# Half of the down projection by seven block products for eight, and a quarter of the up projection's low weight parts by ScalarE and an accumulating transfer

## The chip, the core and the metric

The kernel runs on one core of a Trainium2 chip. The metric is the device time of one launch in microseconds (us). Names used below: PE is the matrix engine TensorE, PEld its weight load, DVE is VectorE, ACT is ScalarE, POOL is GpSimd, SP is SyncE, which issues the loads. SBUF is the memory on the chip that all engines work from, PSUM the memory that matmuls write to.

## The reference, cut to what matters

Two layers, 256 tokens, model width 2048, hidden width 5632, all in float32:

```
x = x + group outputs @ w_out          # two kinds of attention, not touched here
h = rms_norm(x, g2)
u = h @ w_up                           # 2048 -> 2 x 5632 (gate and value)
u = depthwise conv of width 3 over the tokens, per channel, plus bias
m = silu(u[gate]) * u[value]           # 256 x 5632
x = x + m @ w_down                     # 5632 -> 2048
```

The change touches the last line (the down projection), the intermediate m, and the way in which a part of w_up is made ready.

## The kernel before, in words

**Three products for one.** PE multiplies in a format with fewer bits than float32 (fp32r). So each float32 operand is split into a high part, which ACT writes as a rounded copy (L104, in `split`), and a low part, which DVE writes as the difference of the operand and its high part (L105). A product is then high by high, plus low by high, plus high by low. `three` (L388) issues these for the projections in which the tokens' tile is PE's stationary operand and the weights, 512 columns wide, move past it; `two` is the form of the up projection, in which the weights are stationary and a 512-wide matmul (both parts of the activations) is followed by a 256-wide one (the weights' low part).

**Steps.** All weights pass through one pipe. They arrive as tiles of 1 MB (`raw`, 128 partitions by 2048), one tile a *quantum*, by SP's queue in three buffers (`load`); a quantum has two halves, each a *step*: 128 by 1024 weights, split by one instruction on ACT (`whi`) and one on DVE (`wlo`), used by 12 matmuls of `three` or 16 of `two`. `whi` and `wlo` have five buffers each; `split_w` is called four steps ahead of the matmuls. The load of a later quantum goes into a `raw` buffer when the last split of the quantum in it is done.

**Order in a layer.** Input projection, attention, output projection; then the hidden width, cut into 44 tiles of 128 (f = 0 to 43), in chunks (`CHUNKS`, 12, 12, 12 and 8 tiles). For every f of a chunk the up projection takes two quanta (u = 0, 1; 64 matmuls) and `glu` follows: ACT copies the PSUM result (L505), DVE adds its second half (L506) and scales by the norm into a `halo` tile (L507), POOL copies the tile's edges (L509, L510), ACT and DVE do the convolution (L515, L517, four times), ACT the SiLU (L519), DVE the gate (L520), and `split` makes `mid`, the high and low part of m's tile. A chunk's down projection comes after the up projection of the *next* chunk's first tile, so that a `glu` runs beside matmuls that do not need its result; it goes over four column blocks nb of 512, for each over the chunk in groups of four tiles (`q_down`), and adds the PSUM sum to the residual `x` on DVE (`add_x`, L453). In the last chunk of 8, behind which there is no up projection, the order is sorted: both column blocks nb = 0, 1 take the first four tiles, then both take the last four.

**What sets the order.** The program is written as one list of steps, and a scheduler (Tile) orders each engine's instructions by a cost model and by priorities; `split_w` has a raised priority, and so has the last `glu`. Each engine then works through its own list in that order, and waits at an instruction until its inputs and its output buffer are ready. PSUM has 8 banks: two tiles of two banks under the name mm, two of one bank under S, and one each of one bank under tr and pv.

Of the kernel before, what the change touches and what calls it, by code (L numbers as in the profile page):

```python
# [11 lines left out]
F32 = mybir.dt.float32  # L12
# [21 lines left out]
CHUNKS = (12, 12, 12, 8)  # L34
# [17 lines left out]
def encoder_kernel(  # L52
# [91 lines left out]
    def stat_x(which):  # L144
        v = work.tile([P, TT], F32, name="ssum", bufs=2)
        nc.vector.reduce_sum(v, st["ss"], axis=AX.X)
        st["r1"] = act.tile([P, TT], F32, name="r1")
        rsqrt(v, 1.0 / D, st["r1"], "c2")
        if which == 1:

            d = work.tile([P, 4, HD], F32, name="tq", bufs=2)
            for tt in range(TT):
                nc.vector.tensor_scalar(d[:, tt], ident, st["r1"][:, tt:tt + 1], None, op0=ALU.mult)
            ps = psum.tile([P, T], F32, name="pv", bufs=1)
            mm(ps, ones, d[:, 0:TT].rearrange("p t d -> p (t d)"), True, True)
            st["r2"] = act.tile([P, T], F32, name="r2")
            nc.scalar.activation(st["r2"], ps, AF.Copy)
# [199 lines left out]
    def values(l, grp, h):  # L357
# [14 lines left out]
        os[k] = act.tile([P, 2, T], F32R, name="mid", bufs=16)  # L372
# [128 lines left out]
    def glu(l, f, ps):  # L501
# [49 lines left out]
    for l in range(L):  # L551
        for j in range(NJ):
            for u in range(4):
                quanta.append((a["w_in"][l, j, u], q_win(l, j, u), False))
        for grp in "ba":
            for nb in range(NB):
                for u in range(2):
                    quanta.append((a["w_out"][l, 0 if grp == "a" else 1, nb, u], q_wout(l, grp, nb, u), False))
        f = 0
        for c, nf in enumerate(CHUNKS):  # L560

            end = min(sum(CHUNKS[:c + 1]) + 1, NF)
            while f < end:
                for u in range(2):
                    quanta.append((a["w_up"][l, f, u], q_up(l, f, u), True))
# [13 lines left out]
    def load(q, parts=1):  # L579
        if q < len(quanta):  # L580
            raw[q] = wp.tile([P, 2048], F32, name="raw", bufs=3)
            left[q] = 2
# [3 lines left out]

    def split_w(s, parts=1):
        if s < len(steps):
            q, half = steps[s]
            at_ = UP_AT if quanta[q][2] else 0  # L590
            hl[s] = tuple(wp.tile([P, 1024 + 64], F32R, name=t, bufs=SPLIT_AHEAD + 1)[:, at_:at_ + 1024]
                          for t in ("whi", "wlo"))
            m = 1024 // parts
            for j in range(parts):
                with tc.high_priority(offset=AHEAD_PRIO if s >= KD // 2 else 0):
                    highs[s] = split(*(t[:, j * m:(j + 1) * m] for t in hl[s]),
                                     raw[q][:, half * 1024 + j * m:half * 1024 + (j + 1) * m])
# [7 lines left out]
    for i in range(KD // 2):  # L605
        xT.append(act.tile([P, 2, T], F32, name="mid", bufs=16))
# [91 lines left out]
def _layout(inputs):  # L698
# [29 lines left out]
        L, NF, 2, P, 2048)  # L728
    o["w_down"] = c(f["w_down"].reshape(L, NF // FG, FG, P, NB, 512).transpose(0, 1, 4, 3, 2, 5)).reshape(
# [40 lines left out]
```

## Time and profile before

| | |
|---|---|
| three runs | 2125.97, 2126.24 and 2126.32 us, median 2126.24 |
| the profiled execution | 2126.1 us, of which the instructions span 2124.3 |
| PE busy | 2118.1 us, 10904 matmuls |
| DVE busy | 1458.0 us (69% of the span), 2293 instructions |
| ACT busy | 1141.2 us (54%), 1651 instructions |
| POOL busy | 142.1 us (7%), 215 instructions |
| HBM read | 393.93 MB |

A row of the groups has the line, the engine, the operation with output and inputs, shapes, the count; then the busy time in all and the mean time of one in ns; then the idle time of the engine just before these instructions and what ended it. Since instructions on one engine overlap a little, two in a row take less than twice the duration of one.

### The profile page before, as it was taken

What the parts mean: (1) busy time and instruction counts of PE and PEld (TensorE: products, weight loads), DVE (VectorE), ACT (ScalarE), POOL (GpSimd) and SP (SyncE); (2) the same over time, 40 slices, a digit from 0 to 9 for tenths busy, and PEclk for the clock granted to TensorE, in tenths of its full rate; (3) what the DMA queues carried; (4) which work ended last, traced back from release to release, by engine and by line L of the source; (5) the groups of instructions that cost most, each with busy time, mean ns of one, the idle gap of its engine ahead of it and who ended that gap; (6) DMA issues with size and microseconds to landing.
All of it is one profiled execution on the core that took longest, in us unless ns stands there. A gap on an engine that the chain in (4) does not pass through costs nothing.

```text
span 2124.3 us, 28802 instructions
## 1 busy us (share of the span) xinstructions
PE 2118.1 (100%) x10904; PEld 1815.3 (85%) x10904; DVE 1458.0 (69%) x2293; ACT 1141.2 (54%) x1651; POOL 142.1 (7%) x215
## 2 busy tenths in 40 slices
PE   9999999999999999999999999999999999999999
PEld 8888888888888888888888888888888888888887
DVE  7777667775677577657756866677756775776575
ACT  7566556554455355535655665565544553555453
POOL 0000000110011011001000000001100100110010
PEclk9999999999999999999999999999999999999999
DMA  9544555555555555555555454555555555555554
GB/s 345 195 141 170 176 178 178 181 197 198 181 196 191 189 195 182 196 198 182 196 180 197 139 171 160 174 182 185 197 194 184 195 188 192 193 185 197 192 185 139
DMA packets 60843, 397.89 MB, mean 187 GB/s; under 512 B 7328, under 2 KB 9888, under 8 KB 13728
## 3 DMA queue, kind: packets, MB, share of 16 engines
q1 hardware_dynamic: 59696, 394.71, 54.3%
q8 instruction: 85, 1.39, 0.3%
q10 hardware_dynamic: 1008, 1.34, 0.2%
q14 instruction: 54, 0.44, 0.1%
HBM read 393.93 MB, written 2.10 MB: 186 GB/s over the span
## 4 chain that ended last, share of the span: by engine, by line
PE 99%; DMA 0%; ACT 0%; DVE 0%; ACTq 0%; DVEq 0%; issue 0%
PE mm L86 95%; PE pv L86 1%; PE S L86 1%; PE tr L292 1%; PE S L140 0%; PE tr L353 0%; PE tr L86 0%; DMA ln_g<-in_ln_g 0%; PE tr L348 0%; PE tr L345 0%; DVE x L546 0%; ACT xs L107 0%; ACT whi L104 0%; ACTq L608 0%; DVEq L765 0%
## 5 line engine op out<-in xcount | busy, mean ns | idle before, releaser
L105 DVE TENSOR_TENSOR wlo<-raw,whi 128x1024 fp32r<-128x1024 f32 (+1 forms) x737 | 901.2, 1223 | 543.8 <-ACT whi L104 504.9
L104 ACT ACTIVATE whi<-raw 128x1024 fp32r<-128x1024 f32 (+1 forms) x737 | 779.7, 1059 | 863.1 <-PE mm L86 671.9
L86 PE MATMUL mm<-xs,whi 128*128 128x512 f32 x2816 | 976.6, 390 | 0.0
L86 PE MATMUL mm<-xs,wlo 128*128 128x256 f32 x2816 | 794.1, 282 | 0.0
L86 PEld LDWEIGHTS mm<-xs,whi 128*128 128x128 f32 x2816 | 528.3, 188 | 110.5
L86 PEld LDWEIGHTS mm<-xs,wlo 128*128 128x128 f32 x2816 | 532.2, 189 | 0.8
L86 PE MATMUL mm<-whi,mid 128*128 128x512 f32 x1920 | 481.5, 391 | 0.0
L86 PEld LDWEIGHTS mm<-whi,mid 128*128 128x128 f32 x1920 | 357.9, 188 | 72.7
L86 PE MATMUL mm<-whi,xs 128*128 128x512 f32 x1152 | 296.3, 395 | 0.7 <-ACT whi L104 0.7
L86 PE MATMUL mm<-wlo,mid 128*128 128x512 f32 x960 | 260.0, 390 | 0.0
L86 PEld LDWEIGHTS mm<-whi,xs 128*128 128x128 f32 x1152 | 214.6, 188 | 45.4 <-ACT whi L104 1.4
L86 PEld LDWEIGHTS mm<-wlo,mid 128*128 128x128 f32 x960 | 180.0, 188 | 37.2
L86 PE MATMUL mm<-wlo,xs 128*128 128x512 f32 x576 | 162.0, 396 | 0.0
L517 DVE SCALAR_TENSOR_TENSOR pT<-halo,conv,pT 128x256 f32<-128x256 f32 x352 | 146.7, 479 | 0.5
L86 PEld LDWEIGHTS mm<-wlo,xs 128*128 128x128 f32 x576 | 107.3, 188 | 21.7 <-DVE wlo L105 0.4
L509 POOL COPY halo<-halo 128x6 f32<-128x6 f32 x88 | 22.7, 258 | 1359.8 <-DVE halo L507 1359.8
L515 ACT ACTIVATE pT<-halo,conv 128x256 f32<-128x256 f32 x176 | 95.1, 588 | 0.2
L510 POOL COPY halo<-halo 128x6 f32<-128x6 f32 x88 | 95.1, 1081 | 0.2 <-POOL halo L509 0.2
L507 DVE TENSOR_TENSOR halo<-prob,r 128x512 f32<-128x512 f32 x88 | 60.9, 692 | 2.7
L506 DVE TENSOR_TENSOR prob<-prob,mm 128x512 f32<-128x512 f32 x88 | 59.9, 681 | 0.0
L453 DVE TENSOR_TENSOR x<-x,mm 128x1024 f32<-128x1024 f32 x28 | 34.2, 1221 | 35.3 <-PE mm L86 35.3
L505 ACT ACTIVATE prob<-mm 128x512 f32<-128x512 f32 x88 | 51.1, 581 | 0.0
(129 smaller groups left out, 857.8 us busy)
## 6 DMA issues: line engine op xcount, KB each, us to landing
raw<-in_w_up SPq DMA_DIRECT2D x176, 1024.0 KB, 4.8
raw<-in_w_down SPq DMA_DIRECT2D x88, 1024.0 KB, 4.8
raw<-in_w_in SPq DMA_DIRECT2D x71, 1024.0 KB, 4.9
raw<-in_w_out SPq DMA_DIRECT2D x32, 1024.0 KB, 4.8
bias<-in_bias SPq DMA_DIRECT2D x16, 160.0 KB, 3.8
x<-in_x SPq DMA_DIRECT2D x4, 512.0 KB, 8.9
out<-x SPq DMA_DIRECT2D x6, 256.0 KB, 2.5
mid<-in_xT ACTq DMA_DIRECT2D x4, 256.0 KB, 6.2
```

Source lines behind the costliest of these rows:

```text
L86: nc.tensor.matmul(ps, lhsT, rhs, start=start, stop=stop, skip_group_check=True)
L104: high = nc.scalar.activation(hi, src, AF.Copy)
L105: nc.vector.tensor_sub(lo, src, hi.bitcast(F32))
L292: nc.tensor.transpose(ps[:, j, tt * P:(tt + 1) * P], qn[tt][:, p + j, :], ident)
L453: nc.vector.tensor_add(xv, xv, ps)
L505: nc.scalar.activation(t, ps[:, :, 0], AF.Copy)
L506: nc.vector.tensor_add(t, t, ps[:, :, 1])
L507: nc.vector.tensor_mul(ux[:, :, r:r + T], t, st["r2"][:, None, :].to_broadcast([P, 2, T]))
L509: nc.gpsimd.tensor_copy(ux[:, :, 1:r], ux[:, :, T:T + r - 1])
L510: nc.gpsimd.tensor_copy(ux[:, :, T + r:T + 2 * r - 1], ux[:, :, r + 1:2 * r])
L515: nc.scalar.activation(y[:, j, :], ux[:, j, r:r + T], AF.Identity, scale=w1, bias=b)
L517: nc.vector.scalar_tensor_tensor(y[:, j, :], ux[:, j, o:o + T], w, y[:, j, :], op0=ALU.mult, op1=ALU.add)
```

## The change

**Chunks** are now 8, 8, 8, 8, 8 and 4 tiles. The down projection of an 8-tile chunk has two halves by output column. Columns 1024 to 2047 (nb = 2, 3) go as before by `q_down`. Columns 0 to 1023 form, with a pair of mid tiles and the two halves of the tokens, a product of 2x2 blocks by 2x2 blocks, which is done in Winograd's form of Strassen's scheme: seven block products of sums instead of eight. `q_plain` does the one product that needs no sums of weights (two steps of six matmuls) and adds it to x; `q_seven` does the other six for one pair of tiles, in a quantum of three steps of six matmuls each. Four `q_seven` quanta alternate with four `q_down` quanta. The six sums stay in PSUM for the whole stage, in one mm tile and the banks of S (two), tr and pv; the other mm tile serves `q_plain` and `q_down`. So a chunk of 8 has 12 + 4x18 + 4x24 = 180 matmuls where it had 192, and 9 weight tiles of 1 MB where it had 8; it has 22 steps where it had 16.

**Sums.** `sums_mid` makes four sums of the halves of two mid tiles (DVE, 128x128 each) and two more `mid` tiles from them (two splits), once per pair of tiles. `split_seven` makes three sums of weights in place in `raw` on DVE, one 128x1024 and two 128x512, between the first and the second step's split of a quantum. `add_seven` puts the six PSUM sums into x with eight DVE instructions and one on ACT. m itself now stays in float32 in a buffer named bias, `mid` has 17 buffers for 16, and r2 shares a buffer with acc_b.

**The up projection.** In every quantum whose index is even (half of them), the second half's low part is not made by DVE. ACT writes the high part, and then the negative of it into the low part's tile; POOL's queue then issues a transfer that reads the same 512 KB of w_up again from HBM and adds it to what is in the tile. These are 88 steps, a quarter of the up projection's.

**The end of a layer.** The last chunk has four tiles and goes through the four column blocks in plain order.

```
-CHUNKS = (12, 12, 12, 8)
+PART = 8
+CHUNKS = (8, 8, 8, 8, 8, 4)
+MIDS = 17
...
-            st["r2"] = act.tile([P, T], F32, name="r2")
+            st["r2"] = act.tile([P, T], F32, name="acc_b")
...
-        nc.vector.tensor_mul(t[:, 1, :], t[:, 0, :], y[:, 1, :])
-        gs[f] = act.tile([P, 2, T], F32R, name="mid", bufs=16)
-        split(gs[f][:, 0], gs[f][:, 1], t[:, 1, :])
+        m = work.tile([P, T], F32, name="bias", bufs=2)
+        nc.vector.tensor_mul(m, t[:, 0, :], y[:, 1, :])
+        gs[f] = act.tile([P, 2, T], F32R, name="mid", bufs=MIDS)
+        split(gs[f][:, 0], gs[f][:, 1], m)
+        ms[f] = m
+        if f % 2 and f < NF // PART * PART:
+            sums_mid(f // 2, ms.pop(f - 1), ms.pop(f))
+    ms, ss = {}, {}
+    def sums_mid(p, m1, m2):
+        a, b = slice(0, P), slice(P, T)
+        v = work.tile([P, 4, HD], F32, name="tq", bufs=2)
+        nc.vector.tensor_add(v[:, 0], m1[:, b], m2[:, b])
+        nc.vector.tensor_sub(v[:, 1], v[:, 0], m1[:, a])
+        nc.vector.tensor_sub(v[:, 2], m1[:, a], m1[:, b])
+        nc.vector.tensor_sub(v[:, 3], m2[:, a], v[:, 1])
+        for i in range(2):
+            t = act.tile([P, 2, T], F32R, name="mid", bufs=MIDS)
+            split(t[:, 0], t[:, 1], v[:, 2 * i:2 * i + 2].rearrange("p j n -> p (j n)"))
+            for j in range(2):
+                ss[p, 2 * i + j] = t[:, :, j * P:(j + 1) * P]
+    def q_seven(l, c, i):
+        f = sum(CHUNKS[:c]) + 2 * i
+        p = f // 2
+        a, b = slice(0, P), slice(P, T)
+        def body(q, part, hi, lo):
+            if i == 0 and part == 0:
+                t = psum.tile([P, 2, 512], F32, name="mm", bufs=2)
+                ps = {1: t[:, 0], 6: t[:, 1]}
+                for n, name, k in ((5, "S", 2), (7, "S", 2), (3, "tr", 1), (4, "pv", 1)):
+                    ps[n] = psum.tile([P, 512], F32, name=name, bufs=k)
+                cur["seven"] = ps
+            ps = cur["seven"]
+            hv, lv = (w.rearrange("p (k n) -> p k n", k=2) for w in (hi, lo))
+            todo = (((3, ss[p, 3]), (1, gs[f][:, :, a])),
+                    ((7, ss[p, 2]), (5, ss[p, 0])),
+                    ((4, gs[f + 1][:, :, b]), (6, ss[p, 1])))[part]
+            for j, (n, x2) in enumerate(todo):
+                for x_part, w in ((0, hv), (1, hv), (0, lv)):
+                    mm(ps[n], x2[:, x_part], w[:, j], i == 0 and x_part == 0 and w is hv,
+                       i == PART // 2 - 1 and w is lv)
+            if i == PART // 2 - 1 and part == 2:
+                with tc.high_priority(offset=AHEAD_PRIO):
+                    add_seven(ps)
+        return body
+    def add_seven(ps):
+        t = work.tile([P, 512], F32, name="sqx", bufs=1)
+        x11, x12 = x[:, 0, 0:512], x[:, 0, 512:1024]
+        x21, x_2, x2_ = x[:, 1, 0:512], x[:, :, 512:1024], x[:, 1, 0:1024].rearrange("p (j n) -> p j n", j=2)
+        both = lambda v: v[:, None, :].to_broadcast([P, 2, 512])
+        nc.vector.tensor_add(x11, x11, ps[1])
+        nc.scalar.activation(t, ps[1], AF.Copy)
+        nc.vector.tensor_add(t, t, ps[6])
+        nc.vector.tensor_add(x12, x12, t)
+        nc.vector.tensor_add(x12, x12, ps[3])
+        nc.vector.tensor_add(x_2, x_2, both(ps[5]))
+        nc.vector.tensor_add(t, t, ps[7])
+        nc.vector.tensor_add(x2_, x2_, both(t))
+        nc.vector.tensor_sub(x21, x21, ps[4])
+    def q_plain(l, c):
+        f0 = sum(CHUNKS[:c])
+        def body(q, half, hi, lo):
+            if half == 0:
+                cur["dn"] = psum.tile([P, TT, 512], F32, name="mm", bufs=2)
+            ps = cur["dn"][:, 0]
+            hv, lv = (w.rearrange("p (k n) -> p k n", k=2) for w in (hi, lo))
+            for x_part, w in ((0, hv), (1, hv), (0, lv)):
+                for i in range(2):
+                    mm(ps, gs[f0 + 4 * half + 2 * i + 1][:, x_part, 0:P], w[:, i],
+                       half == 0 and i == 0 and x_part == 0 and w is hv, half == 1 and i == 1 and w is lv)
+            if half == 1:
+                xv = x[:, 0, 0:512]
+                nc.vector.tensor_add(xv, xv, ps)
...
-            ps = banks(("dn", nb), g == 0 and half == 0)
+            ps = cur["dn"] if nf == PART else banks(("dn", nb), g == 0 and half == 0)
...
-            ng = nf // FG
-            order = [(nb, g) for nb in range(NB) for g in range(ng)]
-            if end == NF:
-                order = sorted(order, key=lambda o: (o[0] // 2, o[1], o[0]) if o[0] < 2 else (1, 0, 0))
-            for nb, g in order:
-                quanta.append((a["w_down"][l, sum(CHUNKS[:c]) // FG + g, nb], q_down(l, c, nb, g), False))
-
-
-    steps = [(q, h) for q in range(len(quanta)) for h in range(2)]
+            down = lambda nb, g: (a["w_down"][l, sum(CHUNKS[:c]) // FG + g, nb], q_down(l, c, nb, g), "")
+            if nf == PART:
+                quanta.append((a["w_plain"][l, c], q_plain(l, c), ""))
+                for i in range(PART // 2):
+                    quanta.append((a["w_seven"][l, c, i], q_seven(l, c, i), "seven"))
+                    quanta.append(down(2 + i // 2, i % 2))
+            else:
+                for nb in range(NB):
+                    for g in range(nf // FG):
+                        quanta.append(down(nb, g))
...
+    def split_seven(w, part, hi, lo):
+        hv, lv = (t.rearrange("p (k n) -> p k n", k=2) for t in (hi, lo))
+        if part == 1:
+            nc.vector.tensor_sub(w[:, 1:3], w[:, 1:3], w[:, 2:4])
+            nc.vector.tensor_add(w[:, 3], w[:, 3], w[:, 1])
+            nc.vector.tensor_sub(w[:, 0], w[:, 3], w[:, 0])
+        return split(hv, lv, (w[:, 1::2], w[:, 1:3], w[:, 0::3])[part])
...
+    added = {q for q in range(len(quanta)) if quanta[q][2] == "up" and q % 2 == 0}
...
+                if kind == "seven":
+                    highs[s] = split_seven(raw[q].rearrange("p (k n) -> p k n", k=4), half, *hl[s])
+                elif kind == "up" and half == 1 and q in added:
+                    hi, lo = hl[s]
+                    highs[s] = nc.scalar.activation(hi, raw[q][:, 1024:2048], AF.Copy)
+                    nc.scalar.activation(lo, hi.bitcast(F32), AF.Copy, scale=-1.0)
+                    nc.gpsimd.dma_start(out=lo, in_=quanta[q][0][:, 1024:2048], accum_op=ALU.add)
...
+    four = wd[:, :n * PART * P, :1024].reshape(L, n, PART // 2, 2, P, 2, 512)
+    o["w_seven"] = c(np.stack([four[:, :, :, k, :, m] for k, m in ((1, 0), (1, 1), (0, 1), (0, 0))], 4)).reshape(
+        L, n, PART // 2, P, 2048)
+    o["w_plain"] = c(four[:, :, :, 1, :, 0].transpose(0, 1, 3, 2, 4)).reshape(L, n, P, 2048)
```

Three places where each engine's list of instructions differs. The numbers behind names are the tiles; before and after they are counted differently.

DVE in the first down stage, before: the end of a `glu` (L520 to `mid`), the low parts of the weights, and the addition to x at the end of a column block (here a chunk of 12).

```order
L517 SCALAR_TENSOR_TENSOR pT_4437<-halo0_110,conv_469,pT_4437 128x256 x4
L105 TENSOR_TENSOR wlo_4501<-raw_4371,whi_4500 128x1024
L520 TENSOR_TENSOR prob_4431<-prob_4431,pT_4437 128x256
L105 TENSOR_TENSOR wlo_4519<-raw_4413,whi_4518 128x1024
L105 TENSOR_TENSOR mid_4446<-prob_4431,mid_4446 128x256
L105 TENSOR_TENSOR wlo_4535<-raw_4413,whi_4534 128x1024
L453 TENSOR_TENSOR x_70<-x_70,mm_4453 128x2x512
L105 TENSOR_TENSOR wlo_4554<-raw_4470,whi_4553 128x1024
```

DVE in the first down stage of the changed kernel, around the second quantum of seven products (raw_4020) and the `glu` of the next chunk's first tile.

```order
L109 TENSOR_TENSOR wlo_4142<-raw_4020,whi_4141 128x1024
L521 SCALAR_TENSOR_TENSOR pT_4087<-halo0_110,conv_469,pT_4087 128x256 x2
L680 TENSOR_TENSOR raw_4020<-raw_4020 128x1024
L525 TENSOR_TENSOR bias_4095<-prob_4081,pT_4087 128x256
L681 TENSOR_TENSOR raw_4020<-raw_4020 128x512
L540 TENSOR_TENSOR tq_4522<-bias_4095 128x128
L682 TENSOR_TENSOR raw_4020<-raw_4020 128x512
L109 TENSOR_TENSOR wlo_4152<-raw_4020,whi_4151 128x1024
L109 TENSOR_TENSOR mid_4097<-bias_4095,mid_4097 128x256
L109 TENSOR_TENSOR wlo_4165<-raw_4020,whi_4164 128x1024
L109 TENSOR_TENSOR wlo_4183<-raw_4104,whi_4182 128x1024
L109 TENSOR_TENSOR wlo_4199<-raw_4104,whi_4198 128x1024
```

The three sums of weights stand between the first step's low part and the second's, with parts of a `glu` between them; the high parts of the second and third step (whi_4151, whi_4164, on ACT) read their results.

POOL at the first layer's passage from the output projection (acc_a) to the up projection, before:

```order
L116 TENSOR_TENSOR acc_a_2060<-acc_a_2060,sq_2642 128x256
L509 COPY halo0_110<-halo0_110 128x2x3
L510 COPY halo0_110<-halo0_110 128x2x3
L509 COPY halo1_112<-halo1_112 128x2x3
L510 COPY halo1_112<-halo1_112 128x2x3
```

And after:

```order
L120 TENSOR_TENSOR acc_a_2060<-acc_a_2060,sq_2642 128x256
L703 DMA wlo_3008<-in_w_up 128x1024
L703 DMA wlo_3110<-in_w_up 128x1024
L703 DMA wlo_3238<-in_w_up 128x1024
L513 COPY halo0_110<-halo0_110 128x2x3
L514 COPY halo0_110<-halo0_110 128x2x3
L513 COPY halo1_112<-halo1_112 128x2x3
L514 COPY halo1_112<-halo1_112 128x2x3
L703 DMA wlo_3354<-in_w_up 128x1024
```

After, on ACT, in the up projection of the chunks: L701 and L702 are the high part and its negative, which the transfer waits for.

```order
L509 ACTIVATE prob<-mm 128x512
L108 ACTIVATE mid<-tq 128x256
L701 ACTIVATE whi<-raw 128x1024
L702 ACTIVATE wlo<-whi 128x1024
L519 ACTIVATE pT<-halo_110,conv 128x256 x2
L108 ACTIVATE whi<-raw 128x1024
```

One transfer per tile f now stands on POOL among the copies of the edges, and each copy that stands behind a transfer is reached only when the transfer has been issued, which is after L702.

DVE at the end of a layer, before, from the `glu` of f = 43 (prob_7735) to its `mid` (mid_7750):

```order
L105 TENSOR_TENSOR wlo_7754<-raw_7614,whi_7753 128x1024
L506 TENSOR_TENSOR prob_7735<-prob_7735,mm_7654 128x512
L105 TENSOR_TENSOR wlo_7771<-raw_7614,whi_7770 128x1024
L507 TENSOR_TENSOR halo0_110<-prob_7735,r2_3151 128x2x256
L105 TENSOR_TENSOR wlo_7789<-raw_7675,whi_7788 128x1024
L517 SCALAR_TENSOR_TENSOR pT_7741<-halo0_110,conv_469,pT_7741 128x256 x4
L105 TENSOR_TENSOR wlo_7805<-raw_7675,whi_7804 128x1024
L520 TENSOR_TENSOR prob_7735<-prob_7735,pT_7741 128x256
L105 TENSOR_TENSOR wlo_7823<-raw_7717,whi_7822 128x1024
L105 TENSOR_TENSOR mid_7750<-prob_7735,mid_7750 128x256
```

And after (prob_9516 to mid_9532):

```order
L109 TENSOR_TENSOR wlo_9536<-raw_9394,whi_9535 128x1024
L510 TENSOR_TENSOR prob_9516<-prob_9516,mm_9435 128x512
L109 TENSOR_TENSOR wlo_9553<-raw_9394,whi_9552 128x1024
L511 TENSOR_TENSOR halo1_112<-prob_9516,acc_b_3153 128x2x256
L521 SCALAR_TENSOR_TENSOR pT_9522<-halo1_112,conv_469,pT_9522 128x256 x4
L109 TENSOR_TENSOR wlo_9572<-raw_9456,whi_9571 128x1024
L525 TENSOR_TENSOR bias_9530<-prob_9516,pT_9522 128x256
L109 TENSOR_TENSOR mid_9532<-bias_9530,mid_9532 128x256
```

PE after, where it comes to that tile:

```order
L90 MATMUL mm_9575<-wlo_9475,mid_9323 128x512
L90 MATMUL mm_9575<-whi_9494,mid_9428 128x512
L90 MATMUL mm_9539<-whi_9452,mid_9532 128x512
L90 MATMUL mm_9539<-whi_9452,mid_9428 128x512
L90 MATMUL mm_9539<-whi_9452,mid_9532 128x512
```

The scheduler has put 26 matmuls of the last chunk ahead of the first that reads the last `mid`; before it is 48. Between the first step of this `glu` on DVE (L506, now L510) and its `mid`, two low parts of weights stand where there were four, and one right before it.

More of the change, by code (lines that the diff above doesn't have):

```diff
@@ L371, in values @@
         k = g * NH + h
-        os[k] = act.tile([P, 2, T], F32R, name="mid", bufs=16)
+        os[k] = act.tile([P, 2, T], F32R, name="mid", bufs=MIDS)
         split(os[k][:, 0], os[k][:, 1], ps, par["on_g"][:, l, g, h:h + 1])
@@ L564, in encoder_kernel @@
                 for u in range(2):
[L565 removed]
+                    quanta.append((a["w_up"][l, f, u], q_up(l, f, u), "up"))
                 f += 1
[L567 to L575 removed]
+            down = lambda nb, g: (a["w_down"][l, sum(CHUNKS[:c]) // FG + g, nb], q_down(l, c, nb, g), "")
[8 more added lines that the diff above has]
+                        quanta.append(down(nb, g))
+    steps = [(q, h) for q in range(len(quanta)) for h in range(3 if quanta[q][2] == "seven" else 2)]
     raw, hl, left, loads, highs = {}, {}, {}, {}, {}
@@ L581, in load @@
             raw[q] = wp.tile([P, 2048], F32, name="raw", bufs=3)
-            left[q] = 2
+            left[q] = 3 if quanta[q][2] == "seven" else 2
             m = 2048 // parts
@@ L605, in encoder_kernel @@
     for i in range(KD // 2):
-        xT.append(act.tile([P, 2, T], F32, name="mid", bufs=16))
+        xT.append(act.tile([P, 2, T], F32, name="mid", bufs=MIDS))
         if i < 4:
```

23 lines of the change are left out of this document (14 added, 9 removed).

## The prediction

> **What bounds the kernel now.** I read the page's busy times, slices and chain first, then PE's waits, then the groups, then windows on the stages that change.
>
> ```profile
> PE 2118.1 (100%) x10904; PEld 1815.3 (85%) x10904; DVE 1458.0 (69%) x2293; ACT 1141.2 (54%) x1651; POOL 142.1 (7%) x215
> PEclk9999999999999999999999999999999999999999
> DMA  9544555555555555555555454555555555555554
> GB/s 345 195 141 170 176 178 178 181 197 198 181 196 191 189 195 182 196 198 182 196 180 197 139 171 160 174 182 185 197 194 184 195 188 192 193 185 197 192 185 139
> PE 99%; DMA 0%; ACT 0%; DVE 0%; ACTq 0%; DVEq 0%; issue 0%
> ```
>
> PE is busy in every slice at the full granted clock, and 99% of the chain that ended last is PE. PE's waits for other engines:
>
> ```profile
> PE pv L86 <- DVE halfpi L82: 1.1, 1, 1.1
> PE mm L86 <- ACT whi L104: 0.7, 1, 0.7
> ```
>
> 1.8 us in all. So a matmul less is time less, as long as the weights stay ahead of PE; every wait that the change makes is a pure loss. DVE's and ACT's own time costs nothing yet, and the question is where it begins to.
>
> ```profile
> L105 DVE TENSOR_TENSOR wlo<-raw,whi 128x1024 fp32r<-128x1024 f32 x735 | 899.9, 1225 | 543.8 <-ACT whi L104 504.9 <-PE mm L86 20.1 <-ACT mid L107 12.8
> L104 ACT ACTIVATE whi<-raw 128x1024 fp32r<-128x1024 f32 x735 | 778.5, 1060 | 863.1 <-PE mm L86 671.9 <-issue 124.8 <-ACT pT L515 55.8
> ```
>
> DVE's low parts mostly wait for ACT's high parts, and those for PE to give back a buffer (671.9 of 863.1): the pipe is full and PE sets its pace. Stage by stage (windows: two f of the up projection, the last three column blocks of a down stage of 12 tiles, the end of layer 0; the window's length, then PE, PEld, DVE, ACT, POOL busy, clock, DMA share, GB/s):
>
> ```profile
> 448.00:470.20 22.20, 22.20 (x129) 19.67 (x128) 16.82 (x25) 12.65 (x18) 2.75 (x4) 1.00 0.57 193
> 495.33:544.30 48.97, 48.97 (x217) 40.54 (x216) 25.46 (x21) 19.16 (x19) 0.00 (x0) 1.00 0.58 195
> 1018.80:1064.50 45.70, 45.70 (x216) 38.02 (x215) 31.43 (x40) 28.06 (x46) 0.31 (x2) 1.00 0.53 184
> ```
>
> DVE is 76% busy in the up projection and 52% in a down stage (25.46 of 48.97).
>
> **The saving.** Matmuls of the down projection:
>
> ```profile
> 484.45 1.98 PE L86 MATMUL mm<-whi,mid 128*128 128x512 f32 x8
> 486.27 1.07 PE L86 MATMUL mm<-wlo,mid 128*128 128x512 f32 x4
> 487.17 1.07 PE L86 MATMUL mm<-whi,mid 128*128 128x512 f32 x4
> ```
>
> A step of 12 starts at 484.45 and the next at 487.17: 2.72 us, 0.2265 each. An 8-tile chunk loses 12 matmuls of 192; ten chunks in two layers lose 120: 120 x 0.2265 = **-27.2 us**. The new matmuls have the same shape (128x128 stationary, 512 moving), so they take the same price. The down window bears it out: 216 matmuls in 48.97 us are 0.2267 each. It is the one term that I take as certain.
>
> **The up projection.** For two f, 22.2 us, DVE loses two low parts of 1.225 and gets `sums_mid` (4 additions of 0.29 and two low parts of 0.42, rows below, 2.0): 16.4 instead of 16.8. ACT gets two negatives of 1.06 and two high parts of 0.40: 12.65 + 2.9 = 15.6. Both lie beside 22.2 of PE, so the step is worth nothing by itself. What hides it is ACT's 6.6 us of idle time in two f; were that gone, each of 88 steps would cost 1.06, 93 us in all.
>
> **Seven-product stages.** New DVE prices, from the groups:
>
> ```profile
> L453 DVE TENSOR_TENSOR x<-x,mm 128x1024 f32<-128x1024 f32 x28 | 34.2, 1221 | 35.3 <-PE mm L86 35.3
> L507 DVE TENSOR_TENSOR halo<-prob,r 128x512 f32<-128x512 f32 x88 | 60.9, 692 | 2.7
> L105 DVE TENSOR_TENSOR mid<-prob,mid 128x256 fp32r<-128x256 f32 x88 | 36.9, 419 | 0.0
> L196 DVE SCALAR_TENSOR_TENSOR tq<-tq 128x128 f32<-128x128 f32 x26 | 7.4, 290 | 0.6
> 1031.92 2.36 DVE L105 TENSOR_TENSOR wlo<-raw,whi 128x1024 fp32r<-128x1024 f32 x2 [1.16 <-PE mm L86]
> ```
>
> The last row is two low parts in 2.36, so one follows another after 2.36 - 1.225 = 1.14. The sums of weights of a quantum cost 1.22 + 2 x 0.69 = 2.6. A `q_seven` and a `q_down` quantum together are 18 + 24 = 42 matmuls, 9.5 us of PE. DVE has five low parts (5.7), the sums (2.6) and half an addition to x (0.6): 8.9. ACT has 5 x 1.06 = 5.3. So DVE is 94% loaded: it keeps up, with 0.6 us to spare in a pair. The `glu` of the next chunk's first tile, with `sums_mid`, falls into the stage's first third, 5.9 more (0.68 + 0.69 + 1.67 + 2 x 0.42 + 2.0): all four spare parts (2.4) and the lead of four steps of six matmuls (5.4 us) have to bear that. `add_seven` (ACT 0.58, then eight instructions of 0.69 or 1.22, 6.5 in all) runs after the last seven products; the next up projection reuses its mm bank after its first three, about 2.6 us, and 16 matmuls (3.6 us) cover them.
>
> But the chain inside a quantum is long: first low part, 128x1024 sum, ACT's second high part; then the two 512 sums, ACT's third high part, its low part. Walking the first stage by these durations from its first matmul on, with the `glu` pieces where the order has them: the first low part of the second quantum is done at 9.5, L680 at 11.4, L681 at 12.4, L682 at 13.2; the second high part at 12.5 where PE asks for it at 13.6; the third at 14.3 where PE asks at 14.5; the two low parts at 14.35 and 15.9 (asked 15.4, 17.7). The margins are 0.2 to 1.1, in the later quanta 0.3 to 1.1. The lower bound is no stall; the upper is 1.9 us for each stage (each of four quanta late by 0.5, about half of one high part). Nearest to the walk is little, but it has margins no wider than a handoff or two: I take 0.6 a stage, **+6**.
>
> **The end of a layer.** Here the cover of the last `glu` is cut. Before, 48 matmuls of the last chunk (10.9 us) stand between f = 43's up matmuls and the first use of its `mid`; now 26, 5.9 us. The `glu`'s pieces:
>
> ```profile
> L505 ACT ACTIVATE prob<-mm 128x512 f32<-128x512 f32 x88 | 51.1, 581 | 0.0
> L506 DVE TENSOR_TENSOR prob<-prob,mm 128x512 f32<-128x512 f32 x88 | 59.9, 681 | 0.0
> L510 POOL COPY halo<-halo x88: 182/1255/1263, 353.9 to 2081.4; 128x6 f32<-128x6 f32 x88
> L515 ACT ACTIVATE pT<-halo,conv 128x256 f32<-128x256 f32 x176 | 95.1, 588 | 0.2
> 1025.82 1.67 DVE L517 SCALAR_TENSOR_TENSOR pT<-halo,conv,pT 128x256 f32<-128x256 f32 x4
> L104 ACT ACTIVATE mid<-prob 128x256 fp32r<-128x256 f32 x88 | 35.5, 403 | 0.0
> 1024.05 0.19 POOL L510 COPY halo<-halo 128x6 f32<-128x6 f32 x1
> ```
>
> From the last up matmul: ACT's high part stands first (to 1.25), the copy to 1.73; DVE's low part to 2.5, the addition to 3.1; a low part that waits for PE's twelfth matmul to 4.3; the scaling to 4.95; POOL's copies (0.19 each, DVE idle as at 1024.05) and ACT's convolution to 5.6; four on DVE to 7.4, a low part to 8.55, the gate to 8.9, the high part of `mid` to 9.33. 9.33 - 5.9 = 3.4, with a handoff 3.5 us of idle PE, twice: **+7**. Below: without the three low parts in the way (3.4) nothing; above: a copy of 1.255 for 0.19 makes it 4.6. Behind the late `mid` PE's queue holds the rest of the chunk, and behind that x's last addition and the next layer's norm, so nothing recovers it. In layer 0 the transposes for the next norm wait for that addition, behind one more low part: **+1**.
>
> **The accumulating transfer.** It is issued by POOL when ACT's negative is there and must land before PE reaches the step. Four steps are one f, 11.1 us (half of the first window); less two ACT instructions of 1.06 and some 0.4 of handoffs they leave 8.6 us for 76 of the 88; the first ones behind a chunk have more. No row shows such a transfer. The nearest:
>
> ```profile
> raw<-in_w_up SPq DMA_DIRECT2D x176, 1024.0 KB, 4.8
> out<-x SPq DMA_DIRECT2D x6, 256.0 KB, 2.5
> x<-in_x SPq DMA_DIRECT2D x4, 512.0 KB, 8.9
> ```
>
> Between 2.5 for 256 KB and 4.8 for 1 MB a plain 512 KB takes 3.3. Above: queued behind two loads of 4.8 it takes 9.6; x's 512 KB took 8.9 in the crowded first slice. Reading its destination doubles the traffic inside, and loads share the engines: I take 5.5, nearer to the uncrowded rows, since an f now moves 2.5 MB in 11.1 us, 225 GB/s (270 with the destination read again) where the first slice has 345. A transfer of 5.5 is hidden under 8.6: **0**. Behind the transfer on POOL stand the next f's edge copies; they wait for L702, which is done well before the next `glu` in the walk. SP's loads wait for ACT's high part of these steps now and not for DVE, which is earlier, not later.
>
> The row of L510 shows POOL held: 1.255 in the median against 0.182. The Trainium skill, "SBUF — State Buffer", section "Who interferes with whom", says that a DVE instruction with two SBUF inputs contends with a GpSimd instruction that reads SBUF, and that GpSimd can be starved while it makes a transfer's descriptors. The copies agree; no run shows a descriptor held. By the rule an issue is held about 1.1 us as the copies are, the transfer counts 6.6 instead of 5.5, and the sum is the same.
>
> **Sum**, on the profiled execution's own 2126.1 (span 2124.3 and 1.8 around it; the median of the runs is 2126.24): 2126.1 - 27.2 + 6 + 7 + 1 = 2112.9, **2113 us**.
>
> **Rivals.**
>
> *DVE sets the pace of the seven-product stages* (the other side). Place: low part, L680, L681, L682, ACT's high part, in order on DVE. It decides once a pair costs over 9.5; at 10% more than the durations (9.8, plus a handoff of 0.3 in the chain) each of four pairs is 0.6 late, 2.6 a stage, 26 us: 2113 - 6 + 26 = 2133. From 1.9 a stage on it is slower than before (2126 less 2107, by ten). For it: 94% load, the `glu` on top, and a 0.2 margin. Against: five buffers even out single delays, and the 2.36 of two low parts in a row shows DVE without gaps where its inputs are there.
>
> *The accumulating transfer is late.* From 8.6 us on, each us costs 76 us; 0.2 beyond loses the whole gain. At 10 us: 2113 + 1.4 x 76 = 2219. For it: 8.9 and 9.6 above; against: 43% of the DMA engines' time is free in the first window.
>
> *All is hidden*, the layer ends partly: 2126.1 - 27.2 + 0 to 5, 2099 to 2104, if the scheduler's order leaves DVE's low parts earlier than I walk.
>
> *The clock drops after the idle time at the layer's end.* Before there is no such idle time, so the full clock of the slices says nothing. If the 22 matmuls (5.0 us) behind each stall ran at half clock, each end would cost 5 more: 2123. The Trainium skill, "TensorE: Matmul & The Clock Gate", Part 1, says that an idle window of about 3.4 us halves the clock, and that as much busy time restores it; no run here shows it yet.
>
> **Chances.** Forecast (2104 to 2120) 0.42; DVE's pace (2120 to 2150) 0.28; transfer late 0.13; all hidden 0.09; clock 0.08. What a measurement can tell is about 0.2%, 4.25 us: faster ends at 2122, slower begins at 2130.5. Faster: 0.42 + 0.09 + 0.05 (pace) + 0.04 (clock) = 0.60; same: 0.07 (pace) + 0.02 (a transfer just late) + 0.04 (clock) = 0.13; slower: 0.16 (pace) + 0.11 (transfer) = 0.27. The range, 2098 to 2150, leaves out most of the late transfer and the tail of the pace, about 0.15, and little below.
>
> **What would show it.** 10784 matmuls instead of 10904. PE's waits: a few us under `mid` at the two layer ends, about 0.6 a stage on whi L108 from the sums; DVE near 94% busy in a window over a seven-product stage. The transfers' time to landing under 8.6 us, and no wait of PE on them. If PE's waits name the DMA or `wlo` of the up projection, the transfer was late; if they name whi or wlo behind L680 to L682 over 1.9 us a stage, DVE was the bound; if the granted clock falls behind an idle of PE, it was the clock.

## The result: 0.75% slower

The changed kernel takes 2142.23 us (median of 5 runs, 2136.41 to 2146.95) where the kernel before takes 2126.24 (2125.97 to 2126.45): a ratio of 1.0075, with a 95% interval of 1.0056 to 1.0093. The forecast was 2113, so the 13 us that were to be gained became 16 us lost. The profiled execution took 2146.95 us with a span of 2145.1, the slowest of the five; before it was 2126.1 and 2124.3.

The busy times, the clock granted to PE in 40 slices (in tenths of its full speed), the traffic, the chain and the accumulating transfers on the page of the changed kernel:

```profile
PE 2109.3 (98%) x10784; PEld 1802.1 (84%) x10784; DVE 1636.7 (76%) x2711; ACT 1310.2 (61%) x1889; POOL 184.2 (9%) x303
PEclk9999999999999999999999999999999999999999
GB/s 344 191 146 163 168 177 227 233 218 253 197 247 226 223 248 198 249 235 220 191 179 194 139 168 163 177 225 237 223 228 196 271 220 235 233 189 268 214 235 127
PE 87%; issue 8%; DMA 4%; ACT 1%; DVE 0%; ACTq 0%; DVEq 0%; POOLq 0%
wlo<-in_w_up POOLq DMA_DIRECT2D x88, 512.0 KB, 7.1
```

The 120 matmuls are gone (10784 for 10904), but PE's share of the chain has fallen from 99% to 87%, and 4% is now a transfer. The slices, 54 us each, are too coarse to show a slower clock of a few us. PE's waits (engine and line, what for: us in all, times, the longest):

```profile
PE mm L90 <- DMA wlo<-in_w_up: 20.4, 7, 4.2
PE mm L90 <- ACT mid L108: 6.0, 2, 3.1
PE mm L90 <- ACT whi L108: 2.6, 2, 2.1
PE pv L90 <- DVE halfpi L86: 1.1, 1, 1.1
PE S L144 <- DVE x L457: 0.9, 1, 0.9
```

Of 88 accumulating transfers seven make PE wait, 20.4 us. Five waits are long, 3.6 to 4.2 us, all behind a seven-product stage. One of them, in the chain of waits (start, length, what), and on PE:

```profile
568.86 33.38 issue
602.25 0.02 POOLq L703
602.26 10.86 DMA wlo<-in_w_up
```
```profile
613.17 0.58 PE L90 MATMUL mm<-xs,wlo 128*128 128x256 f32 x1 [3.70 <-DMA wlo<-in_w_up]
613.55 0.63 PE L90 MATMUL mm<-xs,whi 128*128 128x512 f32 x1
613.97 0.41 PE L90 MATMUL mm<-xs,wlo 128*128 128x256 f32 x1
614.19 0.63 PE L90 MATMUL mm<-xs,whi 128*128 128x512 f32 x1
```

POOL issues the transfer at 602.26, PE needs it at 609.47 (613.17 less the wait of 3.70), and it lands 10.86 us after its issue. What follows is the second loss: a pair of matmuls now takes 0.64 us (613.55 to 614.19) where it took 0.35. The granted clock (the share of its full speed that PE was given) in windows behind each of the five waits and behind the two layer ends (length; PE, PEld, DVE, ACT, POOL busy; clock; DMA share; GB/s; the second row is the same length behind the first):

```profile
613.17:618.30 5.13, 5.13 (x16) 4.46 (x17) 0.33 (x1) 0.25 (x1) 0.00 (x0) 0.50 0.95 302
618.30:623.43 5.13, 5.13 (x31) 4.53 (x31) 2.45 (x2) 1.87 (x2) 0.00 (x0) 1.00 0.37 88
878.90:884.55 5.65, 5.65 (x18) 4.88 (x19) 0.90 (x2) 0.77 (x1) 0.00 (x0) 0.50 0.97 294
1052.48:1058.63 6.15, 6.15 (x15) 4.80 (x16) 0.40 (x1) 1.05 (x1) 0.00 (x0) 0.50 0.09 27
1550.73:1553.57 2.84, 2.84 (x9) 2.45 (x10) 0.57 (x1) 0.00 (x0) 0.00 (x0) 0.50 0.95 300
1815.27:1819.80 4.53, 4.53 (x17) 3.89 (x18) 1.16 (x2) 0.56 (x1) 0.00 (x0) 0.62 0.93 288
2080.75:2086.04 5.29, 5.29 (x16) 4.53 (x17) 1.14 (x2) 0.40 (x1) 0.00 (x0) 0.50 0.93 307
2123.59:2127.00 3.41, 3.41 (x10) 2.67 (x9) 0.00 (x0) 0.00 (x0) 0.00 (x0) 0.50 0.00 0
```

Half clock and half the matmuls, 16 for 31, for 33.0 us in seven windows. The loss is what the clock lacks to 1: 28.5 x 0.50 + 4.5 x 0.38 = 16.0 us. The account of the span: 120 matmuls less, -27.2; PE's idle time (span less busy) 35.8 instead of 6.2, +29.6; the clock, +16.0; together +18.4 of the 20.8 between the spans. 2.4 us I cannot place. The five runs say much the same without the trace: the longer runs have the lower mean granted clock, with one pair out of order.

```
us      2136.41  2141.57  2142.23  2143.45  2146.95
clock    0.996    0.992    0.992    0.993    0.991
```

What the seven-product stage itself did is in one window, from its first matmul to the first of the next up projection (434.80 to 475.64; two matmuls at its edges are counted with it):

```profile
434.80:475.64 40.84, 40.84 (x182) 33.76 (x181) 40.29 (x48) 25.30 (x30) 1.17 (x2) 1.00 0.57 206
```

It takes the 40.8 us that 180 matmuls need, and PE never waits in it, although DVE is busy for 40.29 of them.

### The profile page after: what moved, and what is told of

It reads as the page before. It is cut to its first block, busy times and chain, and to the rows that moved or that the text cites. A ratio compares the mean times of both kernels' runs of the same rounds, so it can differ in the third digit from the quotient of the medians.

```text
span 2145.1 us, 29366 instructions
## 1 busy us (share of the span) xinstructions
PE 2109.3 (98%) x10784; PEld 1802.1 (84%) x10784; DVE 1636.7 (76%) x2711; ACT 1310.2 (61%) x1889; POOL 184.2 (9%) x303
## 4 chain that ended last, share of the span: by engine, by line
PE 87%; issue 8%; DMA 4%; ACT 1%; DVE 0%; ACTq 0%; DVEq 0%; POOLq 0%
PE mm L90 80%; DMA wlo<-in_w_up 4%; PE S L90 3%; PE pv L90 2%; PE tr L90 1%; PE tr L296 1%; PE S L144 0%; PE tr L357 0%; DMA ln_g<-in_ln_g 0%; DVE wlo L109 0%; ACT whi L701 0%; ACT wlo L702 0%; ACT whi L108 0%; DVE pT L521 0%; PE tr L352 0%
## 5 line engine op out<-in xcount | busy, mean ns | idle before, releaser
L109 DVE TENSOR_TENSOR wlo<-raw,whi 128x1024 fp32r<-128x1024 f32 (+1 forms) x709 | 856.6, 1220 | 313.4 <-ACT whi L108 270.7
L108 ACT ACTIVATE whi<-raw 128x1024 fp32r<-128x1024 f32 (+1 forms) x709 | 736.5, 1055 | 560.9 <-PE mm L90 416.1
L90 PE MATMUL mm<-xs,wlo 128*128 128x256 f32 x2816 | 798.4, 284 | 20.5 <-DMA wlo<-in_w_up 20.4
L90 PE MATMUL mm<-whi,mid 128*128 128x512 f32 x1520 | 400.1, 395 | 6.0 <-ACT mid L108 6.0
L90 PEld LDWEIGHTS mm<-whi,mid 128*128 128x128 f32 x1520 | 284.6, 189 | 65.5 <-ACT mid L108 6.9
L90 PE MATMUL mm<-wlo,mid 128*128 128x512 f32 x760 | 216.1, 393 | 0.0
L701 ACT ACTIVATE whi<-raw 128x1024 fp32r<-128x1024 f32 x88 | 93.1, 1058 | 83.8 <-PE mm L90 83.7
L703 POOL DMA_DIRECT2D wlo<-in_w_up x88 | 76.7, 872 | 755.1 <-ACT wlo L702 665.8
L90 PEld LDWEIGHTS mm<-wlo,xs 128*128 128x128 f32 x576 | 107.3, 188 | 21.7 <-DVE wlo L109 0.4
L702 ACT ACTIVATE wlo<-whi 128x1024 fp32r<-128x1024 f32 x88 | 92.8, 1055 | 1.8
L513 POOL COPY halo<-halo 128x6 f32<-128x6 f32 x88 | 33.6, 382 | 613.7 <-DVE halo L511 613.7
L511 DVE TENSOR_TENSOR halo<-prob,acc_b 128x512 f32<-128x512 f32 x88 | 60.5, 688 | 1.7
L510 DVE TENSOR_TENSOR prob<-prob,mm 128x512 f32<-128x512 f32 x88 | 59.8, 679 | 1.7 <-ACT prob L509 1.7
```

Of the source, the lines that this page charges most:

```text
L90: nc.tensor.matmul(ps, lhsT, rhs, start=start, stop=stop, skip_group_check=True)
L108: high = nc.scalar.activation(hi, src, AF.Copy)
L109: nc.vector.tensor_sub(lo, src, hi.bitcast(F32))
L510: nc.vector.tensor_add(t, t, ps[:, :, 1])
L511: nc.vector.tensor_mul(ux[:, :, r:r + T], t, st["r2"][:, None, :].to_broadcast([P, 2, T]))
L513: nc.gpsimd.tensor_copy(ux[:, :, 1:r], ux[:, :, T:T + r - 1])
```

## The experiments

The theory after this profile: the seven products gain what was forecast; the loss is the few transfers that come first behind a stage, and the slow clock behind idle time of PE. All edits are to the changed kernel unless said otherwise. Ratios are to the kernel before, with 95% intervals.

**1. Without the transfer in the first up quantum** (e1_skip)

```
-    added = {q ... if quanta[q][2] == "up" and q % 2 == 0}
+    added = {q ... if quanta[q][2] == "up" and q % 2 == 0 and quanta[q - 1][2] == "up"}
```

> Leaves the accumulating transfer out in the up quantum that follows another kind of quantum (the first one behind a down stage, and the first of a layer); there DVE makes the low part again. Theory (transfers that are issued about 7 us before PE needs them, at the five stage ends where the first up quantum has the even index, cost a wait of 3.6 to 4.2 us each, and PE's clock halves behind each): 18.9 us of PE's waits and about 10.6 us of slow clock go, about 2113 us, at least 22 us under the changed kernel. Rival (DVE was needed to be relieved just there, the late weights only change their name): PE then waits for DVE's wlo at the same five places, and the time stays above 2130.

Measured: 2116.45 us, ratio 0.9952 (0.9937 to 0.9967). PE's waits in its profile:

```profile
PE mm L90 <- ACT mid L108: 6.0, 2, 3.0
PE mm L90 <- DMA wlo<-in_w_up: 3.2, 4, 1.0
```

The long waits are gone, and no half clock is in this profile before the kernel's end. Leaving out 6 of 88 transfers (five behind stages, one at a layer's beginning) is worth 26 us, though DVE has to make these low parts again. The rival falls. The four waits that remain, up to 1.0 us, are for the next transfer behind a stage. The other three runs, at 0.997 and 0.998, took up to 4.6 us longer.

**2. No transfers** (e2_none)

```
-    added = {q ... if quanta[q][2] == "up" and q % 2 == 0}
+    added = set()
```

> No accumulating transfers at all: DVE makes every low part; the seven products stay. Theory (the transfers bring PE nothing, DVE has room in the up projection: 16.4 + 2.45 = 18.9 of 22.2 us for two tiles): like the kernel without the five first transfers, 2111 to 2114, with no PE wait on a DMA. Rival (with the sums DVE is too full without the transfers, they are what makes the seven products possible): PE waits for wlo in the up projection and in the seven-product stages, over 2120.

Measured: 2110.80 us, ratio 0.9929 (0.9914 to 0.9943).

```profile
PE 2094.7 (99%) x10784; PEld 1793.4 (85%) x10784; DVE 1737.5 (82%) x2799; ACT 1223.9 (58%) x1801; POOL 134.8 (6%) x215
PE mm L90 <- ACT mid L108: 6.1, 2, 3.1
PE mm L90 <- ACT whi L108: 1.5, 1, 1.5
```

DVE, 82% busy, keeps up with all low parts. The transfers relieved an engine that did not need it in the up projection; the seven products do not depend on them.

**3. The transfers alone** (e3_only): the kernel before, with the three lines of the added step in its `split_w` and `added` by the same rule

> The kernel before with the transfers alone (88 steps, always in the first quantum of a tile, so always the first behind a down stage); chunks 12, 12, 12, 8 and no seven products. Theory (it is the short steps of six matmuls and the crowd of loads at the end of a seven-product stage that make the first transfer late): lead of about 8.4 us behind steps of 12 matmuls, landing in 7 to 8 us, PE waits under 3 us in all, 2126 to 2130. Rival (a first transfer on POOL's queue after a pause is slow by itself, 10 us or more): waits of 1.5 to 2.5 us at each of six stage ends, 2136 or more.

Measured: 2126.52 us, ratio 1.0001 (0.9992 to 1.0011); landing 5.9 to 8.3 us, 6.7 in the median.

```profile
PE pv L86 <- DVE halfpi L82: 1.1, 1, 1.1
PE mm L86 <- ACT whi L104: 0.4, 1, 0.4
```

No wait on a transfer, though in this kernel every first up quantum behind a stage has one, after a pause of the queue as long as a stage. Behind down steps of 12 matmuls the same transfer is harmless: behind the six stages it lands after 6.5 to 8.0 us, and where it took 8.0 (issue at 935.11) PE's weight load came 9.1 us after the issue. So it is the neighbourhood of the seven-product stage, not the first use of the queue, that makes it late.

**4. Plain copies** (e4_copy)

```
-nc.gpsimd.dma_start(out=lo, in_=quanta[q][0][:, 1024:2048], accum_op=ALU.add)
+nc.gpsimd.dma_start(out=lo, in_=quanta[q][0][:, 1024:2048])
```

> The changed kernel with plain copies in place of the accumulating transfers: the same 512 KB to the same place at the same time, not added to what is there, so the low parts of a quarter of w_up are wrong. Theory (the landing time of 7.1 us in the median and 10 to 11 at the stage ends is that of a transfer that shares the engines with SP's loads; adding costs under 1 us of it): median 6 to 7, first behind a stage 9 to 10.5, waits of 2.5 to 4 us at the same five ends. Rival (reading the destination and adding doubles the transfer's own time): median 4 to 5 us, stage ends under 7.1, no PE wait on a DMA, about 2115.

Measured: 2129.44 us in one run. The times from issue to landing, of the changed kernel and of this one, and this one's wait:

```profile
DMA to landing us min/median/max: 5.5/7.1/11.0
```
```profile
DMA to landing us min/median/max: 3.9/5.3/9.8
PE mm L90 <- DMA wlo<-in_w_up: 11.6, 5, 3.2
```

Neither expectation has the size: adding costs 1.8 us in the median, twice what I allowed. But the slow places stay: up to 9.8 us, and waits of 1.6 to 3.2 us at the same five stage ends. So adding makes a late transfer later; a copy would be late too.

**5. Always in the second quantum** (e6_second)

```
-    added = {q ... if quanta[q][2] == "up" and q % 2 == 0}
+    added, u = set(), 0
+    for q in range(len(quanta)):
+        u = u + 1 if quanta[q][2] == "up" else 0
+        if u and u % 2 == 0:
+            added.add(q)
```

> The changed kernel with the 88 transfers always in the second quantum of a tile f, so that the first one behind a stage is issued and needed two steps (5.6 us) later. Theory (the first transfer is late because its lead spans steps of six matmuls and lands among the crowded loads; two steps more are enough): no PE wait on a DMA over 1.2 us, under 8 us in all, no slow clock behind them, 2112 to 2117. Rival (the crowd of loads behind a stage delays whichever transfer comes first, lead or not): waits of 2 us or more at the stage ends, 2125 or more.

Measured: 2111.93 us, ratio 0.9933 (0.9919 to 0.9948). All 88 transfers are there, and

```profile
PE mm L90 <- ACT mid L108: 6.0, 2, 3.0
PE mm L90 <- DMA wlo<-in_w_up: 1.3, 1, 1.3
```

One wait on a transfer is left, 1.3 us against an expected 1.2 at most; landing times still go up to 10.2. The wait that is left lies inside an up projection (issue at 1830.90, landing 9.6 us later). Behind the ten stages the transfers land after 8.4 to 10.2 us, and PE asks for them 10.4 to 10.7 us after the issue: the longer lead covers the crowd. Against no transfers at all, 2110.80, they still bring nothing.

**6. How near DVE is to its limit in a stage** (e7_more): without transfers, and two instructions of 128x512 more per quantum of seven products

```
             nc.vector.tensor_sub(w[:, 0], w[:, 3], w[:, 0])
+            nc.vector.tensor_add(w[:, 0], w[:, 3], w[:, 0])
+            nc.vector.tensor_sub(w[:, 0], w[:, 0], w[:, 3])
```

> Without the accumulating transfers, and with two more DVE instructions of 128x512 (1.38 us) in each of the 40 quanta of seven products, which undo each other. Theory (DVE is as full in a stage as counted, 40.25 us busy of 40.8 in the run without transfers, so 5.5 us more in a stage cannot be hidden beyond the lead): PE waits for whi or wlo of 1 to 4 us in each stage, 2120 to 2150. Rival (DVE has slack that its busy time does not show, since it works ahead in the up projection): no new wait, 2110 to 2113.

Measured: 2192.10 us in one run, 81 us over experiment 2 and beyond the expected range.

```profile
PE pv L90 <- ACT whi L108: 51.5, 34, 2.3
```

55 us more on DVE make PE wait 51.5 us, and most of the rest of the 81 goes with a slower clock (0.990 on the mean). Almost every added us is paid: some 0.4 us of 5.5 are hidden per stage (5.5 less 5.15). But this doesn't show that DVE's load is the limit. The added instructions write what the third step's high part reads, so they lengthen the chain inside a quantum too. In the first stage (434.72 to 483.45), and among DVE's waits in it:

```profile
434.72:483.45 48.73, 43.38 (x182) 34.39 (x181) 44.63 (x55) 24.47 (x30) 0.91 (x2) 0.96 0.45 167
DVE wlo L109 <- ACT whi L108: 2.4, 2, 1.2
```

DVE is busy for 44.63 of 48.73 us and itself waits for ACT's high part; in the same stage of experiment 2 it waited for 0.2 us in all. This points to the chain. What load DVE could bear at a place outside the chain was not tested. The rival of the prediction in which DVE sets the pace, at these very instructions, is not what happened, but the stage had little room for it.

**7. The last glu covered by a whole stage** (e5_end): without transfers

```
-            end = min(sum(CHUNKS[:c + 1]) + 1, NF)
+            end = NF if c >= len(CHUNKS) - 2 else sum(CHUNKS[:c + 1]) + 1
...
-        gs[f] = act.tile([P, 2, T], F32R, name="mid", bufs=MIDS)
+        late = f > NF // PART * PART
+        gs[f] = (work if late else act).tile([P, 2, T], F32R, name="qtok" if late else "mid", bufs=3 if late else MIDS)
```

> Without the accumulating transfers, and with the up projection of the last three tiles (f = 41 to 43) moved ahead of the fifth seven-product stage; their mid tiles use three buffers that only the attention needs. So the last glu runs beside a whole stage instead of 26 matmuls. Theory (the two waits of 3.0 us on mid at the layer ends and the slow clock behind them are all that the short last chunk costs): 6 us of waits and about 2.6 us of slow clock less than without the transfers alone (2110.8), 2101 to 2104, and PE's waits under 4 us in all. Rival (the chain only moves: the next norm waits for x at the layer's end, or the stage, with DVE nearly full, pays for what it takes over): 2108 or more, with a PE wait of 2 us or more at another place.

Measured: 2108.35 us, ratio 0.9915 (0.9899 to 0.9932): the rival. The waits on `mid` are gone and two others stand in their place:

```profile
PE mm L90 <- DVE x L457: 3.3, 1, 3.3
PE mm L90 <- DVE x L632: 2.7, 1, 2.7
```

The last chunk's first column block has to be added to x, columns 0 to 511, before its PSUM banks can be used again, and that addition has its place on DVE behind the instructions of `add_seven`, which write the same columns and come late. At the end of layer 0, the last of `add_seven` and, right behind it, the addition that PE waits for until 1041.94 (two additions in one row):

```profile
1039.98 0.68 DVE L590 TENSOR_TENSOR x<-x,pv 128x512 f32<-128x512 f32 x1
1040.57 2.35 DVE L457 TENSOR_TENSOR x<-x,mm 128x1024 f32<-128x1024 f32 x2
```

**8. Its column blocks in another order** (e8_order): as 7, and

```
-                for nb in range(NB):
+                for nb in (2, 0, 1, 3):
...
-    def square_x(nb):
-        if nb == 0:
+    def square_x(nb, fresh):
+        if fresh:
```

> As the run with the last three tiles' up projection ahead of the fifth stage, and the last chunk's column blocks in the order 2, 0, 1, 3: so the first sum that has to leave PSUM goes to columns that add_seven does not write, and is not queued behind it on DVE. Theory (the waits of 3.3 and 2.7 us on x there came from that queue): both gone, PE's waits under 5 us in all, no slow clock, 2100 to 2104. Rival (DVE is behind after the stage, whatever comes first): a PE wait of 2 us or more remains there, 2106 or more.

Measured: 2104.43 us, ratio 0.9898 (0.9883 to 0.9913), 21.7 us under the kernel before and the fastest here.

```profile
PE S L144 <- DVE ssum L150: 1.4, 1, 1.4
PE mm L90 <- ACT whi L108: 1.2, 1, 1.2
PE pv L90 <- DVE halfpi L86: 1.1, 1, 1.1
PE mm L90 <- ACT xs L111: 0.5, 1, 0.5
```

4.2 us of waits in all. It was DVE's queue at that place, not DVE as such.

**9. Work for PE while it waits** (e9_fill): without transfers, in the last chunk's first column block, ahead of its second step

```
+            if nf < PART and nb == 0 and half == 1:
+                idle = psum.tile([P, 512], F32, name="pv", bufs=1)
+                for _ in range(16):
+                    mm(idle, gs[f0][:, 0, 0:P], hv[:, 0], True, True)
```

> The run without transfers, with 16 matmuls more (3.6 us, their results are not used) among the 26 that stand ahead of the last mid at each layer end, so that PE works where it waited 3.0 us. Theory (the half clock follows idle time of PE): no wait on mid, no half clock at the layer ends, granted clock 0.999 or more in every run, and although 32 matmuls are added the time is 1 to 2 us under that without transfers, about 2109. Rival (the half clock comes from something else at these places): it is still there in some runs, and the time is 1 us above, about 2112.

Measured: 2106.71 us, ratio 0.9909 (0.9892 to 0.9925). 32 matmuls more, and 4 us faster than experiment 2. Its four runs lie between 2106.57 and 2106.83, all at a granted clock of 1.000; those of experiment 2 lie between 2109.67 and 2113.29, at 0.997 to 0.999. PE's waits, of which none is at a layer's end:

```profile
PE mm L90 <- ACT whi L108: 1.6, 1, 1.6
PE pv L90 <- DVE halfpi L86: 1.1, 1, 1.1
```

The half clock follows PE's idle time, and it is also what scatters the runs.

## Why the prediction was wrong

**The saving: right.** The stages repeat exactly: without transfers the first sum of a stage begins every 129.6 us (436.9, 566.5, 696.1 on PE), which is eight times 11.1 and 40.8. So -27.2 stands, to about 2 us: in experiment 8, with no half clock before its end, PE is busy for 2092.7 us, 25.4 less than before.

**The seven-product stage: +6 forecast, 0 measured.** PE waits in none of the ten stages, so the margins that I walked held. DVE was busier than the 94% that I expected of a stage, 40.29 of 40.84 us, and experiment 6 shows how little room the chain had. Of the walk's bounds, four times 0.5 is 2.0 and not 1.9 a stage; nothing hangs on it.

**The end of a layer: +7 and +1 forecast, 6.0 and 0.9 measured**, as a wait of 3.0 us on `mid` (forecast 3.5) and one on x. The slow clock behind it was left to a rival.

**The accumulating transfer: 0 forecast, +20.4 measured. This is the step that failed**, and in two of its parts. The landing time was 7.1 us instead of 5.5, which by itself would have been hidden. But the window of 8.6 us, and "the first ones behind a chunk have more", were read from the up projection and from the first stage alone. A stage now has nine weight tiles, an odd number, so that the even indices fall on a tile's second quantum behind one stage and on its first behind the next. At the second kind the four steps of lead are one of six matmuls, two of twelve and one of sixteen: POOL issued at 602.26 and PE asked at 609.47, 7.2 us; at the other four such places it asked after 6.4. So the first ones had less time, not more. And these are the transfers that meet the loads of a stage's end:

```profile
598.00:614.00 16.00, 11.76 (x54) 9.45 (x53) 14.54 (x16) 9.49 (x10) 1.75 (x2) 0.92 0.91 287
```

The DMA engines are busy 91% of these 16 us at 287 GB/s; they were at 57% in the up projection of before, on which I judged the traffic. Landing there takes 9.9 to 10.9 us, beyond my upper bounds of 8.9 and 9.6 (the 9.6 counted two loads ahead and left out the transfer itself). I had the risk and placed it in a rival that made all 76 transfers late at once, 2219 us; the case of five late ones was not among my cases. Both parts count. By an estimate from these numbers, the landing alone, against a lead of 8.6, would have cost 1.3 to 2.3 us a place, and the lead alone, against a landing of 7.1, up to 0.7; together they cost 3.6 to 4.2. Behind the other five stages of the same run the landing takes 8.5 to 9.8 us, PE asks 10.5 to 10.7 us after the issue, and PE does not wait for it; experiment 5 gives all ten that lead. That SP's loads make the landing long is read from the windows; no run took the loads away.

**The clock: 0 forecast, +16.0 in the profiled run.** The rival had the right mechanism, about 5 us for each layer end. The seven stretches cost 2.3 on the mean (3.1 and 1.7 at the two layer ends), and five of the seven were behind the transfers, where the rival saw none. On the trace the half clock ends 3.41 or 6.83 us after it began. The Trainium skill, "TensorE: Matmul & The Clock Gate", Part 1, has a window of about 3.4 us for both directions; the lengths agree with it, but the runs here halve the clock after less idle time, too (last section).

Put together: 2113 - 6 - 1 + 20 + 16 = 2142 with the clock of the profiled run, which took 2147; 5 us are missing, the 2.4 above and about as much in small waits. That the median run took 2142 too is chance: it lost less to the clock, 0.992 for 0.991. The range of 2098 to 2150 held the time by luck: its upper part was there for DVE's pace, which cost nothing. The sign did not hold, because two terms that I set to zero, 20 and 16 us, add up, and 11 of the 16 follow from the 20.

## What to carry to other kernels

When a step is given a longer way to its data, find the place where its lead is shortest, and count it in the time of the steps before it, not in steps: a rule on an index (every even one) lands on different places when the number of steps in a stage changes. A wait of PE of 3 us costs more than itself where the clock halves behind it; filling it with matmuls whose results nobody needs can be a gain. And relieve an engine only where it is late: here DVE was full in the down stages and was relieved in the up projection.

## What the runs showed of the hardware

- The clock does not need a wait of 3.4 us. Of the twelve waits of 2.9 to 3.1 us on `mid` at layer ends in the changed kernel and in experiments 1, 2, 4, 5 and 6, eight were accompanied by a half clock and four were not; in experiment 4 one wait of 2.2 us was too (two of 2.3 were not), and in experiment 6 some of those of 1.8 to 2.3. None of 1.5 us or less was. In the wait shown above, from 609.47 to 613.17, windows of 0.25 us have the clock at 0.50 from 611.5 on, 2.0 us after PE ran dry. Whether a wait between 1.8 and 3.3 us counts looks like a matter of where it falls; that was not tested apart.
- A 512 KB transfer on POOL's queue that adds to its destination takes 7.1 us in the median beside SP's loads, a plain copy 5.3; POOL's own instruction takes 0.87 us for the one and 0.53 for the other.
- POOL is not held at the issue: the 88 issues take 0.862 to 1.011 us beside a busy DVE, where its edge copies vary from 0.18 to 1.25. The Trainium skill, "SBUF — State Buffer", section "Who interferes with whom", warns of GpSimd being starved while it makes descriptors, but says that a probe did not show it beside `tensor_tensor`, which most of DVE's instructions here are; the trace agrees.
